# Down's seven products in another order, the residual loaded in two parts, and one row of steps through gate, up and down

## The chip, the cores and the metric

One core of one Trainium2 chip runs the whole program. The metric is the device time of one execution in microseconds (us). Before the change it is 1949.96 us, the median of three runs (1948.24 to 1951.97).

## The reference, cut to what matters

The program is one layer of a hybrid encoder trunk, with 1024 tokens, 1024 channels and a feed-forward width of 4096. Three mixers and a first layer norm make x1. All that this document is about comes behind that:

```
x  = layer_norm(ALPHA * x + mix @ w_out, ln1_g, ln1_b)          # x1
ff = square(relu(x @ w_up)) @ w_down                            # up, down
pe = sigmoid(x @ w_pe_gate) * (p @ w_pe_proj)                   # gate
x  = layer_norm(ALPHA * x + ff + pe, ln2_g, ln2_b)              # output
```

## The kernel before

**Arithmetic.** Every float32 operand of a matmul is split in two parts, hi (written by ScalarE, L1204 or L866) and lo (the rest, a subtraction in `split_lo`, L116, on VectorE or GpSimd). `three` (L983) then makes three matmuls of one product: hi with hi, hi with lo, lo with hi (L986 to L988). Gate, up and down are each cut in 2x2 blocks and computed with seven block products in place of eight, numbered 1 to 7. Their operands are sums and differences of blocks, their results accumulate in PSUM. Products 1, 6, 7, 4 add up in one set of four banks (`al_`, tag "m"), products 2 and then 5, 3 in the other (`be_`, tags "pj" and "fj"). A running sum is read after each product, before the next product may write its bank. The eight banks are these two sets.

**Gate** (`pg_prep`, `pg_mm`, L1031 to L1082): the products in the order 1, 2, 5, 6, 7, 4, 3, four steps each. Product 5 leaves its sum of weights in a tile `sc` that products 6 and 3 read again (L1037). When a block is done, `pg_fin` loads two tiles (L1001, L1003), takes the sigmoid, multiplies, adds the residual and stores to `xr_d` (L1007). The stage's working tiles lie in the pool "pg".

**Up** (`up_load`, `up_prep`, `up_mm`, L1090 to L1172): 16 column pairs j of 256 columns, seven products each, of 12 matmuls. The raw weights of an even j go into two slots of the general pool (30 slots of 4 KB), those of an odd j into the tile "wur" of a pool "ff" (L1093), which takes the memory of "pg" once the tiles there are released. Results are squared and stored to `h_d` (L1132).

**Down** (`operands`, `down_prep`, `down_mm`, L1178 to L1301): two chunks `ch` of the width, seven products each in the order of the gate, four steps u each, of 24 matmuls, so 96 matmuls a product. `operands` loads raw tiles (six buffers) or cached ones (slots), combines them on VectorE (1024 elements wide) and splits them into hi and lo tiles, of which there are three buffers each; only the last product of the last chunk (`final`) has slots of its own for them and does its matmuls token tile by token tile. After a product `acc` (L1246) adds the four banks to the residual tiles `x2`, in the second chunk with `bn_stats` (L1296) where a half row is complete, and `ln2_t` does the layer norm of a token tile: GpSimd (L190), ScalarE (L1254), four VectorE operations (L1255, L1256), two stores (L1257). All eight `x2` tiles are loaded by the first step of the first product 2 (L1265).

**What sets the order.** Each stage calls `ahead` (L1022), which issues the preparation of step i+3 (gate, up) or i+2 (down) before the matmuls of step i, and ends before the next stage begins. The framework then fixes each engine's order at compile time, by the order of the code and by a model of time, so that a later instruction can be moved ahead of an earlier one that the model sees waiting. On the chip every engine's queue runs in that fixed order. All transfers are issued by SyncE's queue (SPq).

```python
    ahead([(lambda n=n, k=k: pg_prep(n, k), lambda w, n=n, k=k: pg_mm(n, k, w)) for n in ORDER for k in range(4)], 3)
    ff = phase("ff", "tile")
...
    ahead([(lambda j=j, n=n: up_prep(j, n), lambda w, j=j, n=n: up_mm(j, n, w)) for j, n in steps2], 3)
...
    dn = phase("down", "tile")
```

Of the kernel before, what the change touches and what calls it, by code (L numbers as in the profile page):

```python
# [15 lines left out]
P = 128  # L16
# [38 lines left out]
def hybrid_block(ctx, tc, x, xT, pT, w_in, relb, conv_w, conv_b, cln_g, cln_b, dnw, a_log, dt_bias,  # L55
# [975 lines left out]
    def pg_prep(n, k):  # L1031
        if n == 1:
            w = gload(0, 0, k, n)
        elif n == 2 or n == 3:
            w = gload(1, 0, k, n)
            if n == 3:
                V.tensor_tensor(w, w, sc[k], ALU.subtract)  # L1037
        elif n == 5:
            a, b = gload(0, 1, k, n), gload(1, 1, k, n)
            w = sc[k] = pg([P, 512], F32, "sc", 4, "sc")  # L1040
            V.tensor_tensor(w, a, b, ALU.add)
        elif n == 6:
            a = gload(0, 0, k, n)
            w = sc[k]
            V.tensor_tensor(w, w, a, ALU.subtract)
        elif n == 7:
            a, w = gload(0, 0, k, n), gload(0, 1, k, n)
            V.tensor_tensor(w, a, w, ALU.subtract)
        else:
            w = gload(1, 1, k, n)  # L1050
        return hilo(w, f"wg{n}{k}", G if k % 2 else V)
# [27 lines left out]
                pg_fin(4 + t, 0, u2[t])  # L1079

    ORDER = (1, 2, 5, 6, 7, 4, 3)
    ahead([(lambda n=n, k=k: pg_prep(n, k), lambda w, n=n, k=k: pg_mm(n, k, w)) for n in ORDER for k in range(4)], 3)  # L1082


    ff = phase("ff", "tile")
    v4 = lambda a: a.rearrange("p (k c) -> p k c", c=P)
    upo, upa, upb, upc, upr = {}, {}, {}, {}, {}
    NP = DFF // 256

    def up_load(j):  # L1090
        if j >= NP:
            return
        raw = [slot([P, 4, 256], name=f"wu{j}{q}") if j % 2 == 0 else ff([P, 4, 256], F32, "wur", 2, f"wu{j}{q}")  # L1093
               for q in range(2)]
        for q in range(2):
            SY.dma_start(raw[q], wview(w_up, 4 * q, 4, 256 * j, 256))
        upo[j] = (raw[0][:, :, 0:P], raw[1][:, :, 0:P], raw[0][:, :, P:256], raw[1][:, :, P:256])

    ss_ = {}

    def up_prep(j, n):
        a11, a12, a21, a22 = upo[j]
        if n == 1:
            up_load(j + 1)
            src, eng = a11, V
        elif n == 2:
            src, eng = a12, G
        elif n == 4:
            src, eng = a22, G
        else:  # L1110
            t = lraw(f"s{n}")
            src, eng = v4(t), G if n in (6, 3) else V
            if n == 5:
                V.tensor_tensor(src, a21, a22, ALU.add)
                ss_[j] = src
            elif n == 6:
                V.tensor_tensor(src, ss_[j], a11, ALU.subtract)
                ss_[j] = src
            elif n == 7:
                V.tensor_tensor(src, a11, a21, ALU.subtract)  # L1120
            else:
                V.tensor_tensor(src, a12, ss_[j], ALU.subtract)
        hi, lo = hilo(src, f"wu{n}", eng, v4)
        return [(v4(hi)[:, k, :], v4(lo)[:, k, :]) for k in range(4)]

    def ustage(name):
        return ff([P, 512], F32, "st", 10, name)

    def hstore(j, i, hf, v):
        f = 2 * j + i  # L1130
# [34 lines left out]
            steps += [(j + 1, 1), (j + 1, 2)]  # L1165
        steps += [(j, 4), (j, 3)]

    up_load(0)
    steps2 = []
    for j, n in steps:  # L1170
        steps2.append((j, {6: 5, 5: 6}.get(n, n)))
    ahead([(lambda j=j, n=n: up_prep(j, n), lambda w, j=j, n=n: up_mm(j, n, w)) for j, n in steps2], 3)  # L1172
    scoped[0].close()
    scoped[0] = None
    late.close()


    dn = phase("down", "tile")  # L1178
    x2 = [None] * NT

    def dt4(dt, tag, bufs, name):
# [7 lines left out]
    def bload(dst, g, i, j):  # L1189
        SY.dma_start(dst, wview(w_down, 4 * g + 2 * i, 2, 512 * j, 512))  # L1190
        return dst

    def raw():
        return dt4(F32, "raw", 6, "draw")

    def cache(name):
        return slot([P, 2, 512], name=name)

    def hilo4(src, which, final):
        if final:  # L1200
            hi, lo = [slot([P, 2, 512], F32R, name=which + x) for x in "hl"]
        else:
            hi, lo = [dt4(F32R, which + x, 3, which + x) for x in "hl"]
        S.activation(hi, src, AF.Copy)  # L1204
        split_lo(V, lo, src, hi)
        return hi, lo
# [52 lines left out]

    ADDS = {1: [(0, 0)], 2: [(0, 0)], 5: [(1, 1)], 6: [(0, 1)], 7: [(1, 1)], 4: [(1, 0)], 3: [(0, 1)]}  # L1260
    def down_prep(ch, n, u):
        if (ch, n, u) == (0, 2, 0):
            for t in range(NT):
                x2[t] = slot([P, D], name=f"x2_{t}")
                SY.dma_start(x2[t], xr_d[t])  # L1265
        if (ch, n, u) == (1, 1, 0):
            rows.extend([load_rows(ln2_g), load_rows(ln2_b)])
        return operands(n, 4 * ch + u, (ch, n) == (1, 3))

    rows, held = [], []  # L1270

    def down_mm(ch, n, u, ab):
# [2 lines left out]
        if n in (2, 5) and u == 0:  # L1275
            be_[:] = [bank(ALT[t], name="pdb") for t in range(4)]
        bs = al_ if n in (1, 6, 7, 4) else be_
        final = (ch, n) == (1, 3)
        if final:
            held.append(ab)  # L1280
        else:
# [7 lines left out]
        for t in range(4):  # L1289
# [2 lines left out]
                    for k in range(2):  # L1292
                        three(bs[t], part(a, k, t), part(b, k), False, v == 3 and k == 1)
            acc(4 * i + t, c, bs[t])
            if ch == 1 and n in (2, 7, 4, 3):
                V.bn_stats(lst[4 * i + t][:, c, :], x2[4 * i + t][:, 512 * c:512 * c + 512])  # L1296
                if n in (4, 3):
                    ln2_t(4 * i + t, *rows)

    ahead([(lambda ch=ch, n=n, u=u: down_prep(ch, n, u), lambda ab, ch=ch, n=n, u=u: down_mm(ch, n, u, ab))  # L1300
           for ch in range(2) for n in ORDER for u in range(4)], 2)  # L1301
    scoped[0].close()


# [37 lines left out]
```

## Time and profile before

| | us |
|---|---|
| median of 3 runs | 1949.96 |
| the profiled execution, its own time | 1944.56 |
| its span, first to last instruction | 1942.8 |
| gate, up and down with the last layer norm, in that span | about 1169 to 1943 |
| up's first matmul | 1275.2 |
| down's first matmul | 1601.0 |

The profiled execution lies 0.28% under the median of the runs. Times in the rows are microseconds from the span's start. A matmul's own time is longer than the distance to the next, since matmuls overlap; lengths of products are therefore taken from start to start. In the names, pga and pgb are the two bank sets in gate, pua, pub and puc the banks in up, pda (`al_`) and pdb (`be_`) the sets in down.

### The profile page before, as it was taken

The page shows a single profiled execution, that of the slowest core. Times are in us where ns is not written, and L with a number is a line of the kernel's source. Part 1 is how long each engine was busy: PE and PEld are TensorE (multiplying, and loading weights), DVE is VectorE, ACT ScalarE, POOL GpSimd, SP SyncE. Part 2 cuts the span into 40 slices and gives each one's busy share as a digit, 9 for nine tenths or more (in the row PEclk, how much of TensorE's full clock was granted, in tenths as well). Part 3 has the DMA queues.
Part 4 walks back from the last instruction along what each step waited for, and adds up shares of the span by engine and source line. Part 5 has one row for each costly group of instructions (what it writes and reads, how often), then busy time and mean ns, then how long its engine had stood idle before and what let it go on. Part 6 is the DMA issues. An engine that isn't in the chain of part 4 may idle for free. (4 is left out here: it accounts for less than half of the span.)

```text
span 1942.8 us, 25812 instructions
## 1 busy us (share of the span) xinstructions
PE 1850.1 (95%) x9265; PEld 1543.4 (79%) x9265; DVE 1258.3 (65%) x2203; ACT 831.1 (43%) x1516; POOL 445.0 (23%) x373
## 2 busy tenths in 40 slices
PE   8999999989999989989999999989999989999996
PEld 7988887778777878777877997768888877878775
DVE  3248969989957857664377367763333327865978
ACT  4454544446324343442344237435555553333333
POOL 2123423334322122212121142223232310000001
PEclk9999999999999989999999999999999999999998
DMA  6212222232242332333354435763333367542442
GB/s 200 82 53 68 74 64 72 65 87 87 87 117 60 98 90 84 92 111 107 125 190 163 155 123 188 246 211 130 104 114 108 109 233 251 214 162 97 175 152 87
DMA packets 207793, 244.68 MB, mean 126 GB/s; under 512 B 23792, under 2 KB 126256, under 8 KB 207664
## 3 DMA queue, kind: packets, MB, share of 16 engines
q1 hardware_dynamic: 207664, 243.03, 38.6%
q8 instruction: 73, 1.20, 0.2%
q14 instruction: 56, 0.46, 0.1%
HBM read 183.17 MB, written 59.80 MB: 125 GB/s over the span
## 5 line engine op out<-in xcount | busy, mean ns | idle before, releaser
L676 DVE SCALAR_TENSOR_TENSOR ca<-ci,cw_s,ca 128x512 f32<-128x512 f32 x240 | 214.2, 892 | 3.8
L986 PE MATMUL pda<-bh,ah 128*128 128x512 f32 x256 | 97.6, 396 | 9.1 <-DVE x L1246 5.1
L987 PE MATMUL pda<-bl,ah 128*128 128x512 f32 x256 | 100.6, 393 | 0.0
L988 PE MATMUL pda<-bh,al 128*128 128x512 f32 x256 | 100.4, 393 | 0.0
L190 POOL TENSOR_TENSOR mv<-mv,nhalf 128x1 f32<-128x1 f32 x16 | 17.4, 1094 | 360.9 <-DVE mv L683 360.9
L307 POOL TENSOR_SCALAR st<-st,mx 128x640 f32<-128x640 f32 (+2 forms) x64 | 58.7, 919 | 179.8 <-DVE mx L306 174.2
L304 ACT ACTIVATE st<-st,mx 128x640 f32<-128x640 f32 (+2 forms) x64 | 44.5, 696 | 117.0 <-DVE mx L300 116.8
L986 PE MATMUL pdb<-bh,ah 128*128 128x512 f32 x192 | 74.6, 401 | 7.0 <-DVE x L1246 7.0
L1204 ACT ACTIVATE ah<-draw 128x1024 fp32r<-128x1024 f32 x32 | 33.9, 1061 | 102.9 <-PE pda L987 51.2
L1157 DVE TENSOR_TENSOR r<-puc,r 128x512 f32<-128x512 f32 x16 | 11.1, 692 | 103.1 <-PE puc L988 103.1
L987 PE MATMUL pdb<-bl,ah 128*128 128x512 f32 x192 | 76.4, 398 | 0.0
L988 PE MATMUL pdb<-bh,al 128*128 128x512 f32 x192 | 75.9, 398 | 0.0
L986 PEld LDWEIGHTS pda<-bh,ah 128*128 128x128 f32 x256 | 48.6, 190 | 20.9 <-ACT bh L1204 7.3
L988 PEld LDWEIGHTS pda<-bh,al 128*128 128x128 f32 x256 | 48.7, 190 | 10.4
L987 PEld LDWEIGHTS pda<-bl,ah 128*128 128x128 f32 x256 | 48.7, 190 | 10.2 <-DVE bl L116 0.2
L553 DVE TENSOR_TENSOR tm<-X 32x31 f32<-32x31 f32 (+15 forms) x124 | 53.4, 431 | 3.0
L116 DVE TENSOR_TENSOR al<-draw,ah 128x1024 fp32r<-128x1024 f32 x32 | 39.1, 1221 | 22.7 <-ACT ah L1204 22.7
L431 DVE SCALAR_TENSOR_TENSOR c<-pc,dnw_s,c 128x511 f32<-128x511 f32 (+2 forms) x72 | 52.5, 731 | 0.1
L554 DVE TENSOR_TENSOR X<-X,tm 32x31 f32<-32x31 f32 (+15 forms) x124 | 50.1, 404 | 3.0
L771 ACT ACTIVATE sgl<-sgl 128x512 f32<-128x512 f32 x48 | 30.2, 631 | 50.0 <-DMA sgl<-sg_d 41.5
L334 ACT ACTIVATE ph<-tp 128x512 fp32r<-128x512 f32 (+2 forms) x72 | 37.0, 525 | 32.0 <-PE tp L330 27.5
L116 POOL TENSOR_TENSOR wu2l<-wu,wu2h 128x512 fp32r<-128x512 f32 x16 | 20.8, 1303 | 128.1 <-ACT wu2h L866 128.1
(1605 smaller groups left out, 6199.7 us busy)
## 6 DMA issues: line engine op xcount, KB each, us to landing
draw<-h_d SPq DMA_DIRECT2D x48, 512.0 KB, 5.0
wu<-in_w_up_dram SPq DMA_DIRECT2D x32, 512.0 KB, 3.9
h_d<-r SPq DMA_DIRECT2D x64, 256.0 KB, 2.1
draw<-in_w_down_dram SPq DMA_DIRECT2D x32, 512.0 KB, 4.6
sg_d<-fs SPq DMA_DIRECT2D x48, 256.0 KB, 2.1
sgl<-sg_d SPq DMA_DIRECT2D x48, 256.0 KB, 2.8
wg<-in_w_pg_dram SPq DMA_DIRECT2D x36, 256.0 KB, 4.3
cb<-in_w_down_dram SPq DMA_DIRECT2D x16, 512.0 KB, 8.1
```

What stands on the lines that cost most here:

```text
L116: eng.tensor_tensor(lo, src, hi.bitcast(F32), ALU.subtract)
L304: S.activation(st[:, :nk], st[:, :nk], AF.Exp, scale=-1.0, bias=mx[:, nm:nm + 1], accum_out=mx[:, 2:3])
L307: G.tensor_scalar(st[:, :nk], st[:, :nk], mx[:, 3:4], 1.0, ALU.mult, ALU.mult)
L334: S.activation(ph[:, :n], tp[:, :n], AF.Copy)
L431: V.scalar_tensor_tensor(acc[:, 512 * hf + s_:512 * hf + 512], pp[:, :512 - s_], cw[:, 3 - s_:4 - s_], acc[:, 512 * hf + s_:512 * hf + 512 ...
L553: V.tensor_tensor(tv, bc_last(L, ncol), bc_mid(R, nr), ALU.mult)
L554: V.tensor_tensor(X3[:, jj + 1:32, 0:ncol], X3[:, jj + 1:32, 0:ncol], tv, ALU.subtract)
L676: V.scalar_tensor_tensor(acc, t[:, H - s_:H - s_ + 512], cw_s[:, i, H - s_:KB - s_], acc, ALU.mult, ALU.add)
L986: PE.matmul(out_, lhsT=ah, rhs=bh, start=first, stop=False, skip_group_check=True)
L987: PE.matmul(out_, lhsT=ah, rhs=bl, start=False, stop=False, skip_group_check=True)
L988: PE.matmul(out_, lhsT=al, rhs=bh, start=False, stop=last, skip_group_check=True)
L1204: S.activation(hi, src, AF.Copy)
```

## The change

- Down's products come in the order 2, 1, 5, 6, 3, 7, 4. So the last one, with slots of its own, is product 4 in place of 3; the layer norm of token tiles 0 to 3 follows product 3, that of tiles 4 to 7 follows product 4.
- Residual tiles 0 to 3 are loaded by the first step of product 1, tiles 4 to 7 by the third step of product 5.
- The three calls of `ahead` become one row of steps: preparations of up are issued during gate's last steps, those of down during up's last. Up loses its pool "ff": "wur" moves into "pg" and shares its two buffers of 4 KB with gate's `sc` (two `sc` tiles in each), its staging tiles use "st" of "pg", with 12 buffers in place of 10.
- Down's pool is opened only when it is first needed. The first two steps of product 2 in chunk 0 take raw, hi and lo tiles from the general slots.

```diff
         elif n == 5:
             a, b = gload(0, 1, k, n), gload(1, 1, k, n)
-            w = sc[k] = pg([P, 512], F32, "sc", 4, "sc")
+            if k % 2 == 0:
+                sc[k] = pg([P, 1024], F32, "wur", 2, "sc")
+                sc[k + 1] = sc[k][:, 512:]
+                sc[k] = sc[k][:, :512]
+            w = sc[k]
...
-    ff = phase("ff", "tile")
...
-        raw = [slot([P, 4, 256], name=f"wu{j}{q}") if j % 2 == 0 else ff([P, 4, 256], F32, "wur", 2, f"wu{j}{q}")
+        raw = [slot([P, 4, 256], name=f"wu{j}{q}") if j % 2 == 0 else v2(pg([P, 1024], F32, "wur", 2, f"wu{j}{q}"))
                for q in range(2)]
...
     def up_prep(j, n):
+        if n == 1:
+            if j == 0:
+                up_load(0)
+            up_load(j + 1)
...
-        return ff([P, 512], F32, "st", 10, name)
+        return pg([P, 512], F32, "st", 12, name)
...
+    dnp = []
+
+    def dn(*a):
+        if not dnp:
+            scoped[0].close()
+            scoped[0] = None
+            late.close()
+            dnp.append(phase("down", "tile"))
+        return dnp[0](*a)
...
+    first = [False]
+
     def raw():
-        return dt4(F32, "raw", 6, "draw")
+        return cache("raw") if first[0] else dt4(F32, "raw", 6, "draw")
...
-        if (ch, n, u) == (0, 2, 0):
-            for t in range(NT):
+        if ch == 0 and (n, u) in ((1, 0), (5, 2)):
+            for t in range(4 if n == 5 else 0, 8 if n == 5 else 4):
                 x2[t] = slot([P, D], name=f"x2_{t}")
                 SY.dma_start(x2[t], xr_d[t])
-        if (ch, n, u) == (1, 1, 0):
+        if (ch, n, u) == (1, 3, 0):
             rows.extend([load_rows(ln2_g), load_rows(ln2_b)])
-        return operands(n, 4 * ch + u, (ch, n) == (1, 3))
+        first[0] = (ch, n) == (0, 2) and u < 2
+        return operands(n, 4 * ch + u, (ch, n) == (1, 4) or (ch, n) == (0, 2) and u < 2)
...
-        final = (ch, n) == (1, 3)
+        final = (ch, n) == (1, 4)
...
-            if ch == 1 and n in (2, 7, 4, 3):
+            if ch == 1 and n in (1, 7, 4, 3):
...
+    flow = [([(3, lambda _, n=n, k=k: pg_prep(n, k))], lambda w, n=n, k=k: pg_mm(n, k, w))
+            for n in ORDER for k in range(4)]
+    flow += [([(3, lambda _, j=j, n=n: up_prep(j, n))], lambda w, j=j, n=n: up_mm(j, n, w)) for j, n in steps2]
+    flow += [([(2, lambda _, ch=ch, n=n, u=u: down_prep(ch, n, u))], lambda ab, ch=ch, n=n, u=u: down_mm(ch, n, u, ab))
+             for ch in range(2) for n in (2, 1, 5, 6, 3, 7, 4) for u in range(4)]
+    made = {}
+    for i in range(-4, len(flow)):
+        for lead in (4, 3, 2):
+            if 0 <= i + lead < len(flow):
+                for l, f in flow[i + lead][0]:
+                    if l == lead:
+                        made[i + lead] = f(made.get(i + lead))
+        if i >= 0:
+            flow[i][1](made.pop(i))
```

## Rows read from the trace of the kernel before

**Rows 1.** The page: an engine's busy time, share of the span, instructions.

```profile
PE 1850.1 (95%) x9265; PEld 1543.4 (79%) x9265; DVE 1258.3 (65%) x2203; ACT 831.1 (43%) x1516; POOL 445.0 (23%) x373
```

**Rows 2.** Waits of PE, 1150 to 1943: waiter, releaser, us in total, times, longest.

```profile
PE pua L986 <- ACT wu1h L866: 7.9, 1, 7.9
PE pdb L986 <- DVE x L1246: 7.0, 2, 3.8
PE pda L986 <- DVE x L1246: 5.1, 4, 2.4
PE pda L986 <- ACT bh L1204: 4.0, 1, 4.0
...
PE pub L986 <- DVE u L1078: 1.4, 1, 1.4
```

**Rows 3.** Windows: up's first five products; one later. Busy (count) by engine, PEclk, DMA.

```profile
1275.20:1300.48 25.28, 15.98 (x62) 12.31 (x60) 13.36 (x20) 6.68 (x12) 1.10 (x1) 0.86 0.66 217
1569.89:1572.64 2.75, 2.75 (x14) 2.25 (x13) 0.00 (x0) 0.60 (x1) 1.30 (x1) 1.00 0.92 240
```

**Rows 4.** Timeline of up's beginning: start, us, engine, line, tiles [idle before].

```profile
1290.69 0.68 DVE L1157 TENSOR_TENSOR r<-pub,r 128x512 f32<-128x512 f32 x1
1291.22 2.11 SPq L1096 DMA_DIRECT2D wu<-in_w_up_dram  x2
1291.41 0.63 ACT L1158 ACTIVATE r<-r 128x512 f32<-128x512 f32 x1 [7.91 <-DVE r L1157]
...
1295.24 0.63 ACT L866 ACTIVATE wu1h<-wu 128x512 fp32r<-128x512 f32 x1 [2.54 <-DMA wu<-in_w_up_dram]
...
1297.36 0.63 PE L986 MATMUL pua<-xc1h,wu1h 128*128 128x512 f32 x1
...
1297.79 0.63 PE L987 MATMUL pua<-xc1l,wu1h 128*128 128x512 f32 x1
```

**Rows 5.** Line 1037, gate's last reads of sc: ns min/median/max, first and last start.

```profile
L1037 DVE TENSOR_TENSOR wg<-wg,sc x4: 692/692/694, 1244.7 to 1249.7; 128x512 f32<-128x512 f32 x4
```

**Rows 6.** SyncE's queue, timeline of up's end: the residual's loads.

```profile
1572.60 6.51 SPq L1265 DMA_DIRECT2D x<-xr_d  x6
```

**Rows 7.** Windows of down, PE product starts (1; 2; 5+6; 7; 3; 2; 5+6; 7; 4+3).

```profile
1601.02:1625.58 24.56, 24.56 (x96) 20.02 (x97) 14.91 (x15) 9.79 (x11) 0.00 (x0) 0.88 0.54 191
1625.58:1650.67 25.09, 21.92 (x97) 17.86 (x96) 21.54 (x21) 10.02 (x10) 0.00 (x0) 1.00 0.89 307
1650.67:1696.79 46.12, 45.41 (x193) 37.10 (x193) 40.17 (x40) 14.86 (x15) 0.00 (x0) 0.96 0.59 215
1696.79:1721.27 24.48, 22.04 (x97) 17.94 (x97) 16.29 (x17) 9.15 (x10) 0.00 (x0) 1.00 0.54 182
...
1743.15:1764.91 21.76, 21.76 (x98) 18.02 (x96) 12.18 (x13) 8.05 (x9) 0.00 (x0) 1.00 0.15 50
...
1786.67:1812.41 25.74, 21.92 (x97) 17.86 (x96) 21.44 (x21) 10.02 (x10) 0.00 (x0) 0.98 0.88 310
1812.41:1859.89 47.48, 46.79 (x192) 37.93 (x193) 42.54 (x44) 14.84 (x15) 0.00 (x0) 0.94 0.28 97
1859.89:1883.15 23.26, 22.02 (x96) 17.94 (x97) 16.38 (x17) 8.58 (x10) 0.00 (x0) 1.00 0.54 184
1883.15:1926.85 43.70, 43.70 (x192) 35.93 (x192) 41.08 (x68) 17.81 (x21) 4.14 (x5) 1.00 0.21 69
```

**Rows 8.** Window from the end of the last product 7 to VectorE's last instruction.

```profile
1882.30:1939.20 56.90, 43.86 (x192) 35.96 (x192) 54.22 (x97) 23.11 (x28) 5.90 (x8) 0.93 0.26 91
```

**Rows 9.** VectorE's timeline in that window: neighbours of 1024 and of 512 elements.

```profile
1898.43 1.22 DVE L116 TENSOR_TENSOR bl<-draw,bh 128x1024 fp32r<-128x1024 f32 x1
1899.57 1.22 DVE L116 TENSOR_TENSOR bl<-cb,bh 128x1024 fp32r<-128x1024 f32 x1
...
1921.96 0.67 DVE L1255 TENSOR_TENSOR x<-x,lnp 128x512 f32<-128x512 f32 x1
1922.55 0.68 DVE L1256 TENSOR_TENSOR x<-x,lnp 128x512 f32<-128x512 f32 x1
```

More of the change, by code (lines that the diff above doesn't have):

```diff
@@ L1081, in hybrid_block @@
     ORDER = (1, 2, 5, 6, 7, 4, 3)
-    ahead([(lambda n=n, k=k: pg_prep(n, k), lambda w, n=n, k=k: pg_mm(n, k, w)) for n in ORDER for k in range(4)], 3)
-    ff = phase("ff", "tile")
     v4 = lambda a: a.rearrange("p (k c) -> p k c", c=P)
+    v2 = lambda a: a.rearrange("p (k c) -> p k c", c=256)
     upo, upa, upb, upc, upr = {}, {}, {}, {}, {}
@@ L1101, in up_prep @@
     def up_prep(j, n):
+        if n == 1:
+            if j == 0:
+                up_load(0)
+            up_load(j + 1)
         a11, a12, a21, a22 = upo[j]
         if n == 1:
-            up_load(j + 1)
             src, eng = a11, V
@@ L1166, in hybrid_block @@
         steps += [(j, 4), (j, 3)]
-    up_load(0)
     steps2 = []
@@ L1171, in hybrid_block @@
         steps2.append((j, {6: 5, 5: 6}.get(n, n)))
[L1172 to L1178, printed above, removed]
+    dnp = []
[6 more added lines that the diff above has]
+        return dnp[0](*a)
     x2 = [None] * NT
@@ L1191, in bload, with hilo4 @@
         return dst
+    first = [False]
     def raw():
-        return dt4(F32, "raw", 6, "draw")
+        return cache("raw") if first[0] else dt4(F32, "raw", 6, "draw")
     def cache(name):
         return slot([P, 2, 512], name=name)
-    def hilo4(src, which, final):
-        if final:
+    def hilo4(src, which, own):
+        if own:
             hi, lo = [slot([P, 2, 512], F32R, name=which + x) for x in "hl"]
@@ L1298, in down_mm @@
                     ln2_t(4 * i + t, *rows)
-    ahead([(lambda ch=ch, n=n, u=u: down_prep(ch, n, u), lambda ab, ch=ch, n=n, u=u: down_mm(ch, n, u, ab))
-           for ch in range(2) for n in ORDER for u in range(4)], 2)
+    flow = [([(3, lambda _, n=n, k=k: pg_prep(n, k))], lambda w, n=n, k=k: pg_mm(n, k, w))
[12 more added lines that the diff above has]
+            flow[i][1](made.pop(i))
     scoped[0].close()
```

## The prediction

> **What bounds the kernel now.** I read the page first: PE is busy 95% of the span [rows 1], so time can only come from its waits, or from matmuls that run at the lower clock. The changed stages begin at about 1169 us, so the second view is PE's waits behind that. Five of them lie in places that the change touches [rows 2]: 7.9 and 1.4 us where up begins, 4.0 where down begins, and 12.1 in down (7.0 and 5.1) in which PE waits for `acc` to read a bank that the next product writes. The third view is the windows, because a wait also costs what comes after it. One product of up takes 2.75 us when nothing disturbs it [rows 3], one of down 21.76 us [rows 7]; what a stretch takes above that is its loss, the low clock included.
>
> At up's beginning the cause is in order of time [rows 4]: SyncE issues the loads of the second column pair at 1291.2, behind all loads and stores of gate's `pg_fin`, because their memory was part of gate's pool; ScalarE can split them at 1295.2, and PE then runs at 0.43 us from matmul to matmul, the lower level of 1.2 GHz, where 0.23 is usual. At down's beginning nothing is missing but memory: the operands were loaded, their hi and lo tiles lie where up's tiles lay.
>
> **The change part by part.** The sum is made against the profiled execution, 1944.56 us, which stands 5.4 us below the median of the runs; I carry the difference over to the median.
>
> (a) Up's beginning. The first five products take 25.28 us where 5 x 2.75 = 13.75 would do [rows 3]: a loss of 11.5. The loads of pair 1 now need only the memory of `sc`, whose last reader starts at 1249.7 [rows 5]. They are issued some 40 us earlier, two of 512 KB, and nothing stands behind their wait on SyncE's queue for longer than that subtraction. What is late next: product 2 of pair 0 still waits 1.4 us for gate's banks [rows 2], and product 7 of pair 0 waits for a copy that stands on ScalarE behind L1158 and one square, so it comes at 1291.4 + 3 x 0.63 = 1293.3 [rows 4]. With the five products in a row from 1279.5 (pair 0's 2, 5, 6, pair 1's 1, 2), PE is there at 1279.5 + 13.75 = 1293.25. So 1.7 us stays and 9.8 go. Bounds: 2 gained (the splits of pair 1 queue behind L1157, at 1290.7, and little but the load's wait goes) to 11.5 (all).
>
> (b) Down's beginning. The wait of 4.0 [rows 2] and the first product's 24.56 - 21.76 = 2.8 [rows 7] are 6.8 us. The first two steps now have tiles of their own in slots that up's finished operands free, so they can be ready before up ends. They give PE 2 x 5.44 us; within them the third step's raw tiles must land and be split. Late next is one bank that up's last product leaves to a VectorE read of 0.68 [rows 4], while three others are free. I take the whole 6.8; bounds 3 to 6.8.
>
> (c) Chunk 0. The bank conflicts in the old order are 2 to 5, 6 to 7 and 7 to 4; in the new one 2, 1, 5, 6, 3, 7 each find their bank set unused for a whole product, and only 7 to 4 is left. Losses now: 25.09 - 21.76 = 3.3 (product 2, waiting for the bank at its end), 46.12 - 43.52 = 2.6 (5 and 6: low clock behind that wait, and the wait before 7), 24.48 - 21.76 = 2.7 (7, waiting before 4) [rows 7]. 2.7 stays, 5.9 go. Bounds 3 to 8.6.
>
> (d) Chunk 1, products before the last two. 25.74 - 21.76 = 4.0 and 47.48 - 43.52 = 4.0 [rows 7]: 7.9 go. Bounds 5 to 7.9. Its wait from 7 to 4 (23.26 - 21.76 = 1.5) stays and is counted in (e).
>
> (e) The end. From 1882.3, when the last product but two is done, to the span's end at 1942.8 are 60.5 us, and VectorE is busy 54.2 of the first 56.9 [rows 8]: here it is VectorE that sets the end, not PE, which has only two products (43.70 us) [rows 7] to do. The change does not take an operation from it. From the end of product 3 it has the same list: 16 operations of 1024 elements, 1.14 apart, and about 56 of 512, 0.6 apart, with small ones [rows 9], in all 54 us. What changes is the order. In the code four layer norms (each four operations of 0.6 and three small ones, some 2.7 us) now stand ahead of product 4's twelve splits and subtractions, which PE needs; the old order had half its norms behind all splits. Strictly in the code's order, product 4's last operands are ready after 15.6 (adds, statistics and norms of product 3: 4 x 3.9) + 4.5 (four splits of product 7) + 13.6 (12 x 1.14) + 4.8 (product 7's adds and statistics) + 3 of waits = 41.5 us. PE then still has up to 78 matmuls to do, 17.7 us, and the last tile's norm takes some 8 by my estimate, with 3.6 from VectorE's last instruction to the span's end [rows 8]: 71, a loss of 10. If the norms only fill gaps, PE ends after 43.5 + 1.5 and the end comes at 57: a gain of 4. The nearest row is the old end, where the planner put the splits first; I take a loss of 2.
>
> **Costed at nothing.** The number of loads does not change. Residual tiles 0 to 3 are needed at product 2's end, 21.8 us into down, tiles 4 to 7 two products later; today six issues pass SyncE's queue within 6.5 us during up [rows 6], whose stores they hardly delay. If that cover is gone, `acc` waits on VectorE with the next splits behind it, which two steps of lead (10.9 us) absorb.
>
> Sum: -9.8 - 6.8 - 5.9 - 7.9 + 2.0 = -28.4. On the profiled execution 1916.2, against the median **1921.6, say 1922 us**.
>
> **A rule weighed.** Where one product follows another on the other bank set, from 4 to 3, PE loses nothing: product 3 takes 21.76 us at a granted clock of 1.00 [rows 7]. The Trainium skill, TensorE: Matmul & The Clock Gate, "A second HAM failure mode: psum-queue depth-cycling", warns against what the new order does more often: a kernel that cycled through banks in PSUM lost throughput to brief idling between groups of matmuls and a clock that fell and rose. By that rule part of (c) and (d) would be given back; the row is against it.
>
> **The rivals.**
> - *The norms starve product 4* (the strict order of (e)): 10 lost in place of 2, 1930 us. For it: norms come first in the code. Against it: while ScalarE and GpSimd have a norm in hand, VectorE is free for splits.
> - *Up's beginning stays late*: VectorE's and ScalarE's queues are late next, not the load. (a) gives 2, so 1929 us. For it: ScalarE idles 7.9 us for VectorE [rows 4].
> - *The one row does nothing*: the planner already moves work ahead (the residual's loads run during up [rows 6]), and both seams stay. (a) and (b) are gone: 1922 + 16.6 = 1938 us.
> - *Each change of bank set costs*, as the low clock does behind a wait for a bank: (2.6 - 0.7) in chunk 0 and (4.0 - 0.7) in chunk 1 [rows 7], 2.6 in the mean. Eleven changes are 28.6: 1950 us, no change. For and against it is what the paragraph above says.
> - *Slower*: VectorE starves PE in chunk 1's products 7 and 4 at every step, and PE stays at 1.2 GHz for both. Deficit: 38.5 us of VectorE work (15.6 + 4.5 + 13.6 + 4.8) against some 26 of PE (product 7 and the first tile of 4), 13; and 192 matmuls at 0.43 in place of 0.23, 38.4. In place of the 2 that makes 51: 1971 us. It decides once stalls and low clock pass 30 us, with 13 of stalls from some 85 of the 192 matmuls. For it: behind today's waits the clock is down (0.88 over a product) [rows 7]. Against it: it rose again within that product each time, since operands were there.
>
> **How the numbers follow.** Forecast 60%, norms first 18%, late up 8%, seams stay 5%, bank sets 2%, slower 6%, and 1% for what I have not thought of, put with no change. Only the forecast's own bounds reach far down: all gains at their best are 42, which together is unlikely, so the range begins at 1912. It ends at 1938, with the seams that stay. A measurement of this kernel can tell about 0.2%, 3.9 us. Faster by more: 60 + 18 + 8 + 5 = 91%; within it 3%; slower 6%.
>
> **What would show it.** (a) right: no wait of PE for wu1h, first five products of up in about 15.5 us. (b): no 4 us gap, first product of down near 21.8. (c), (d): `acc` named as PE's releaser only before product 4; 2 to 5 gone. (e): VectorE busy nearly all of the last 60 us, PE with a wait for product 4's splits. A wait of PE of over 5 us in products 7 or 4, or a granted clock under 0.9 there, would make the forecast wrong; so would a PE gap over 4 us at either seam.

## The result and the profile after

The changed kernel takes **1930.41 us** (median of four runs, 1929.69 to 1931.43) beside 1949.85 us before (median of four runs, one more than above; 1948.24 to 1951.97): a ratio of 0.99, 95% interval 0.9883 to 0.9917, so 16 to 23 us less. It lies inside the range of the prediction, 8.4 us above its 1922: 28 us were forecast, 19.4 came.

| us | before | after |
|---|---|---|
| median of the runs | 1949.85 | 1930.41 |
| profiled execution, its own time | 1944.56 | 1930.17 |
| span | 1942.8 | 1928.2 |
| gate's last matmul ends | 1275.4 | 1277.2 |
| up's last matmul ends | 1597.0 | 1597.1 |
| last matmul of the kernel ends | 1927.0 | 1916.8 |

The profiled execution of before stood 5.4 us under its median, that of after stands on its own. So the two traces differ by 14.4 us only. Of these, gate gives back 1.8, and it is not shown to be the change's doing: in the profiles of the experiments below, gate's last matmul ends anywhere from 1274.3 to 1286.1 us in kernels that have the same gate as after or, in e11_x1_bufs, nearly so. So I compare behind gate's last matmul: 667.4 us before, 651.0 after, **16.5 us less**. Against these the steps are counted.

PE's waits from 1150 us on, in the columns of [rows 2]:

```profile
PE pda L986 <- DVE x L1258: 8.3, 2, 4.4
PE pdb L986 <- ACT bh L1216: 5.5, 1, 5.5
PE pub L986 <- DVE u L1082: 2.2, 1, 2.2
...
PE pda L987 <- DVE bl L116: 1.2, 1, 1.2
```

The wait of 7.9 us for wu1h is gone, and of the six waits for `acc` (L1246 before, L1258 now) two are left, both between products 7 and 4. But down's beginning has a longer wait than before (5.5 for 4.0), in its third step in place of its first. The wait of 1.2 us for bl is in product 7 of chunk 1.

Windows of after, in the columns of [rows 3, 7]: up's first five products; down's first 60 matmuls behind up (and two of the next product); chunk 0's products 7 and 4; chunk 1's product 1; its 5 and 6; and from product 7 to the span's end:

```profile
1277.08:1294.82 17.74, 15.58 (x61) 12.33 (x60) 14.33 (x19) 7.36 (x14) 5.10 (x3) 0.90 0.88 302
1597.84:1619.89 22.05, 16.52 (x62) 13.13 (x63) 14.26 (x13) 9.40 (x11) 0.00 (x0) 0.85 0.91 322
1706.48:1755.76 49.28, 45.39 (x194) 37.12 (x192) 34.10 (x35) 16.07 (x17) 0.00 (x0) 0.97 0.56 184
1777.52:1799.28 21.76, 21.76 (x98) 18.02 (x96) 19.50 (x20) 8.05 (x9) 0.00 (x0) 1.00 0.69 250
1799.28:1842.80 43.52, 43.52 (x194) 36.05 (x192) 38.66 (x42) 16.09 (x17) 0.00 (x0) 1.00 0.07 20
1864.56:1928.20 63.64, 46.62 (x193) 37.42 (x191) 58.36 (x100) 23.55 (x28) 8.21 (x8) 0.89 0.38 133
```

A product of up takes 2.75 us undisturbed and one of down 21.76 (0.227 us a matmul). The first row loses 17.74 - 13.75 = 4.0 (11.5 before), the second 22.05 - 62 x 0.227 = 8.0, the third 49.28 - 43.52 = 5.8. The fourth and fifth lose nothing, where before 4.0 and 4.0 were lost [rows 7].

Down's beginning in the trace, SyncE's queue (SPq), ScalarE and PE:

```profile
1592.46 7.00 SPq L1138 DMA_DIRECT2D h_d<-r  x3
1599.55 0.39 SPq L1196 DMA_DIRECT2D draw<-h_d  x1
1600.04 0.45 SPq L1200 DMA_DIRECT2D draw<-in_w_down_dram  x1
...
1603.99 1.06 ACT L1216 ACTIVATE ah<-draw 128x1024 fp32r<-128x1024 f32 x1 [4.87 <-DMA draw<-h_d]
1605.32 1.06 ACT L1216 ACTIVATE bh<-draw 128x1024 fp32r<-128x1024 f32 x1 [0.27 <-DMA draw<-in_w_down_dram]
...
1606.43 2.07 PE L986 MATMUL pdb<-bh,ah 128*128 128x512 f32 x4 [5.53 <-ACT bh L1216]
```

The third step's loads stand on the queue behind up's last three stores of h, which wait there until 1599.46 for the tiles that they store. ScalarE idles 4.87 us for them, PE 5.53. And of the 48 matmuls of the first two steps, meant as cover, 36 had run already between up's last products, from 1572.2 to 1591.4, in place of up's small waits for `r`.

VectorE between products 7 and 4 of chunk 0: the split for product 4's second step, product 4's last subtraction, the four accumulations.

```profile
1727.76 1.22 DVE L116 TENSOR_TENSOR bl<-draw,bh 128x1024 fp32r<-128x1024 f32 x1
1730.32 1.23 DVE L1247 TENSOR_TENSOR draw<-draw,ct 128x1024 f32<-128x1024 f32 x1 [1.34 <-DMA draw<-in_w_down_dram]
1731.46 2.47 DVE L1258 TENSOR_TENSOR x<-pda,x 128x512 f32<-128x512 f32 x4
```

The accumulations, for which PE stands 3.89 us, queue behind the subtraction for product 4's fourth step, which PE comes to 3 x 5.44 us after the first, and which itself waits 1.34 us for its load. (PE began product 7's last step at 1722.80 without a wait, so all splits behind that are product 4's.)

Before the last product 4, in chunk 1, the accumulations stand behind product 4's subtractions and splits and among the norms' scalings (L1267):

```profile
1888.08 1.22 DVE L1247 TENSOR_TENSOR draw<-draw,ct 128x1024 f32<-128x1024 f32 x1
...
1889.81 1.22 DVE L116 TENSOR_TENSOR bl<-draw,bh 128x1024 fp32r<-128x1024 f32 x1
1890.95 0.68 DVE L1267 TENSOR_TENSOR x<-x,lnp 128x512 f32<-128x512 f32 x1
1891.55 0.68 DVE L1258 TENSOR_TENSOR x<-pda,x 128x512 f32<-128x512 f32 x1
```

### The profile page after: what moved, and what is told of

Same layout as the page of the kernel before. It is cut to its first block, busy times and chain, and to the rows that moved or that the text cites. A ratio compares the mean times of both kernels' runs of the same rounds, so it can differ in the third digit from the quotient of the medians.

```text
span 1928.2 us, 25795 instructions
## 1 busy us (share of the span) xinstructions
PE 1848.2 (96%) x9265; PEld 1545.3 (80%) x9265; DVE 1254.8 (65%) x2203; ACT 831.8 (43%) x1516; POOL 449.9 (23%) x373
## 5 line engine op out<-in xcount | busy, mean ns | idle before, releaser
L986 PEld LDWEIGHTS pda<-bh,ah 128*128 128x128 f32 x256 | 49.1, 192 | 19.2 <-ACT x L1266 4.8
L987 PEld LDWEIGHTS pda<-bl,ah 128*128 128x128 f32 x256 | 49.1, 192 | 11.9 <-DVE bl L116 1.7
L431 DVE SCALAR_TENSOR_TENSOR c<-pc,dnw_s,c 128x511 f32<-128x511 f32 (+2 forms) x72 | 52.5, 731 | 0.1
L986 PEld LDWEIGHTS pdb<-bh,ah 128*128 128x128 f32 x192 | 36.4, 190 | 14.6 <-ACT bh L1216 6.0
```

The costliest lines, as they stand in the source:

```text
L431: V.scalar_tensor_tensor(acc[:, 512 * hf + s_:512 * hf + 512], pp[:, :512 - s_], cw[:, 3 - s_:4 - s_], acc[:, 512 * hf + s_:512 * hf + 512 ...
L986: PE.matmul(out_, lhsT=ah, rhs=bh, start=first, stop=False, skip_group_check=True)
L987: PE.matmul(out_, lhsT=ah, rhs=bl, start=False, stop=False, skip_group_check=True)
```

## The experiments

Theory after the result: the change's parts work, but (1) down's beginning depends on where the third step's loads stand on SyncE's queue, (2) the two waits left in down come from the order on VectorE, not from the amount of its work, and (3) order and row of steps need each other. (The planner is the framework's scheduler, which fixes each engine's order.) In the table the "stretch" runs, in the profile, from up's last matmul to the span's end (before 345.8, after 331.1; kernels with the one row, so all but before and e1_order, have 8.2 us of down's matmuls ahead of it).

| kernel | median | before, same chip | ratio, 95% interval | stretch |
|---|---|---|---|---|
| e1_order | 1945.75 | 1947.73 | 0.9985, 0.9974 to 0.9996 | 343.3 |
| e2_row | 1937.70 | 1947.73 | 0.9941, 0.9923 to 0.9960 | 336.4 |
| e3_raw_slots | 1925.20 | 1947.73 | 0.9888, 0.9866 to 0.9909 | 329.8 |
| e6_norm_after | 1932.61 | 1947.73 | 0.9908, 0.9889 to 0.9927 | 334.9 |
| e5_raw7 | 1933.96 | 1947.65 | 0.9921, 0.9899 to 0.9944 | 335.1 |
| e7_no_norm | 1925.26 | 1947.65 | 0.9878, 0.9854 to 0.9901 | 327.7 |
| e8_acc_first | 1927.51 | 1947.65 | 0.9894, 0.9870 to 0.9918 | 327.2 |
| e9_one_part | 1929.47 | 1947.65 | 0.9909, 0.9885 to 0.9932 | 333.6 |
| e10_all | 1924.52 | 1951.68 | 0.9862, 0.9845 to 0.9878 | 322.3 |
| e11_x1_bufs | 1930.06 | 1951.68 | 0.9888, 0.9873 to 0.9902 | 332.3 |
| e12_pool_norm | 1928.39 | 1951.68 | 0.9871, 0.9849 to 0.9893 | 324.7 |
| e13_end_order | 1918.14 | 1946.53 | 0.9850, 0.9830 to 0.9870 | 321.9 |

The ratio is an estimate from all runs and not the quotient of the two medians. The executions of one kernel spread by some 10 us here, so what separates kernels by few us is read from the stretch and its waits.

The stretch has a part that moves without an edit. From the last product 7 to the span's end it takes 63.6 us in after and 63.3 in e11_x1_bufs, but 65.0 to 65.7 in e3_raw_slots, e5_raw7, e8_acc_first, e9_one_part and e10_all, whose end has the same code. In these five VectorE's order is another: in e8_acc_first four and in e10_all three of the norms' multiplications and additions (0.6 us each) stand between the last accumulation and its statistics, in after none. So some 2 us of a stretch can be this order, and each edit is judged by the window that it aims at.

**The order alone.**

```diff
...
-           for ch in range(2) for n in ORDER for u in range(4)], 2)
+           for ch in range(2) for n in (2, 1, 5, 6, 3, 7, 4) for u in range(4)], 2)
```

> The kernel before with the new order of down's products alone (2, 1, 5, 6, 3, 7, 4, with the last product, the norms' rows and the moments moved to fit); gate, up and down keep their three separate rows of steps, and all eight parts of the residual are loaded at down's first step. Theory (the parts lean on each other): the bank waits of down's second half go (7.9 us) and 2.9 us of the first half's, the end costs 2.7 us more, but down now begins with product 2, whose four raw tiles of each step come late behind eight residual loads: down's beginning stays at 24.5 us or gets up to 5 us worse. Sum -3 to -8 us, so 1942 to 1947 against 1950. Rival (the parts are independent, down's beginning doesn't mind which product is first): -8 us. Rival (the single row of steps brings nearly all of the gain): within 2 us of the kernel before, with bank waits as before.

Its gain is 1 to 5 us, at the edge of what was expected. The time alone would also fit the last rival, but the bank waits went as in after (chunk 1 loses nothing, chunk 0 5.7), but down's beginning got 4.3 us worse: 11.2 us are lost in it, 6.9 before.

```profile
1590.21 12.39 SPq L1132 DMA_DIRECT2D h_d<-r  x4
1602.70 0.37 SPq L1186 DMA_DIRECT2D draw<-h_d  x1
...
1609.29 1.22 PE L986 MATMUL pdb<-bh,ah 128*128 128x512 f32 x2 [9.09 <-ACT bh L1204]
```

Product 2's raw tiles lie in down's pool, so their loads go out behind four stores of up and PE waits 9.09 us. Product 1, first in the old order, loads into slots.

**The row alone.**

```diff
...
-             for ch in range(2) for n in (2, 1, 5, 6, 3, 7, 4) for u in range(4)]
+             for ch in range(2) for n in ORDER for u in range(4)]
```

(The cut lines load the residual in one part at product 2 and give the slots for hi and lo tiles to the first two steps of product 1.)

> The changed kernel with down's old order of products (1, 2, 5, 6, 7, 4, 3) and the residual in one part at the first step of product 2; the one row of steps stays. Theory: the gain in up stays (7.5 us at its first five products, 2.7 in its last ones), down's beginning is judged by what its third step waits for: its tiles for product 1 are slots of the cache, free from the start, so their loads can go out ahead of up's last stores of h, the wait of 5.5 us at down's third step goes and 5 to 7 us are gained there; the bank waits are as in the kernel before. Sum -14 to -18 us: 1932 to 1936. Rival (the third step waits for something else than loads queued behind up's stores, such as the splits on ScalarE and VectorE): the 5.5 us wait stays, -9 to -11 us: 1939 to 1941.

Measured 8 to 15 us less than before, in the median (1937.7) between the theory and the rival. The mechanism held: with product 1 first all loads of its four steps are out by 1586.6, the third step's split follows up's last square on ScalarE at once, at 1603.44, and the 5.5 us wait fell to 1.3 and 1.4.

```profile
1586.16 0.42 SPq L1200 DMA_DIRECT2D cb<-in_w_down_dram  x1
...
1602.90 0.63 ACT L1137 ACTIVATE r<-r 128x512 f32<-128x512 f32 x1
1603.44 1.04 ACT L1216 ACTIVATE ah<-ca 128x1024 fp32r<-128x1024 f32 x1
```

```profile
PE pda L987 <- DVE bl L116: 1.4, 1, 1.4
PE pda L986 <- ACT bh L1216: 1.3, 1, 1.3
```

```profile
1601.31:1620.92 19.61, 16.97 (x62) 13.11 (x60) 12.07 (x12) 9.21 (x11) 0.00 (x0) 0.83 0.88 314
```

The size did not: 60 matmuls still take 19.61 us for 13.6, at a granted clock of 0.83, so PE ran at 1.2 GHz for part of them behind two short waits. Order alone and row alone gave 2.9 and 11.5 us (ratios times 1949.85), both together 19.4; behind gate's last matmul the traces show 1.2, 10.6 and 16.5. By the intervals (1 to 5, 8 to 15, 16 to 23) the surplus over the sum is not clear of noise. That the order needs the row, which gives product 2 slots and lead, is read from the traces: down's beginning, where e1_order waits 9.09 us.

**All raw tiles of the first product in slots.**

```diff
-        first[0] = (ch, n) == (0, 2) and u < 2
+        first[0] = (ch, n) == (0, 2)
```

> The changed kernel, with the raw tiles of all four steps of down's first product (not of two) in slots that are free before up ends, so that SyncE issues the third and fourth step's loads ahead of up's last stores of h. Theory (down's third step waits for loads that stand on SyncE behind those stores): the wait of PE for bh of 5.53 us at down's third step falls under 1 us, the low clock behind it goes, 5 to 7 us less than the changed kernel: 1923 to 1926. Rival (the split tiles' buffers or ScalarE's work set it): the loads land earlier, the wait stays at 3 us or more, under 2 us less. Rival (the loads now collide with up's stores or delay them): up's last products wait, no gain.

The loads of down's first product in the trace (count, ns, first and last start), and PE's window over its last 60 matmuls:

```profile
L1200 SPq DMA_DIRECT2D raw<-in_w_down_dram x4: 386/420/422, 1562.3 to 1576.2; - x4
L1196 SPq DMA_DIRECT2D raw<-h_d x3: 360/371/408, 1569.2 to 1575.7; - x3
```

```profile
1601.71:1619.16 17.45, 15.96 (x61) 12.36 (x61) 11.21 (x10) 8.97 (x11) 0.00 (x0) 0.90 0.83 307
```

```profile
PE pdb L987 <- DVE bl L116: 1.3, 1, 1.3
```

They are out before 1577 where the third step's went out at 1599.6. The wait for bh is gone (0.2 us; 1.3 us for bl is left), the loss is 17.45 - 13.6 = 3.8 for after's 8.0. That is the theory, a little short of 5 us (the median, 1925.2, lies in its band), and it repeats: the four kernels with this edit lose 2.4 to 4.7 us in these 60 matmuls, the seven with the one row, the new order and without it 7.5 to 8.5. The stretch is only 1.3 us shorter than after's, since products 7 and 4 of chunk 0 lose 7.0 us here for 5.8 and the end 1.6 more.

The edit gives the loads other memory as well as another place on the queue. That the place counts can be read in after's trace: what the first of the third step's loads waits for had been set by 1588 (for its memory, GpSimd's last instruction, at 1575.3), and it went out at 1599.55. The load for bh, at 1600.04, waits also for PE, at the latest for up's last matmul at 1597.1. So at least 2.9 us of its delay are the queue's; how much of the rest is the memory's is not shown.

**The accumulations of chunk 0 first.**

```diff
-            V.tensor_tensor(b, b, ct[g], ALU.subtract)
+            with tc.issue_after(done7[0]) if g in (2, 3) else ExitStack():
+                V.tensor_tensor(b, b, ct[g], ALU.subtract)
...
```

(`done7` is product 7's last accumulation in chunk 0; what the block issues queues behind it on its engine.)

> The changed kernel with VectorE's subtractions for product 4's third and fourth steps, in down's first half, queued behind product 7's four accumulations instead of ahead of them. Theory B (the wait of 3.9 us between products 7 and 4 there is the order on VectorE): the wait falls to 1.5 us or less, the low clock behind it goes too, 2.5 to 5 us less: 1925.5 to 1928. Theory A (buffers and loads set it; the splits of product 7 stand ahead as well): the wait stays over 2.5 us. Rival (the put-off subtractions starve product 4's later steps): a new wait of 1 to 3 us for bl at its third or fourth step, and no gain.

```profile
1723.61 2.73 DVE L1259 TENSOR_TENSOR x<-pda,x 128x512 f32<-128x512 f32 x4
1726.26 2.35 DVE L1248 TENSOR_TENSOR draw<-draw,ct 128x1024 f32<-128x1024 f32 x2
```

```profile
1703.69:1747.21 43.52, 43.52 (x194) 36.04 (x192) 33.67 (x35) 16.20 (x17) 0.00 (x0) 1.00 0.64 205
```

Products 7 and 4 on the same banks now take 43.52 us: nothing is lost at all, 5.8 gained, and no wait came in its place; the median, 1927.5, lies in theory B's band. This too repeats: in the four kernels with this edit nothing is lost there, in the seven with the new order, the one row and without it 5.8 to 8.9 us. (The stretch is 3.9 us shorter than after's, since the end takes 65.2 us for 63.6.) The rival that one more buffer would do it was tried beside it:

```diff
-        return cache("raw") if first[0] else dt4(F32, "raw", 6, "draw")
+        return cache("raw") if first[0] else dt4(F32, "raw", 7, "draw")
```

> The changed kernel with seven raw buffers for down's loads instead of six. In the changed kernel VectorE's subtraction for product 4's fourth step waits 1.34 us for its load, with product 7's four accumulations queued behind it, and PE stands 3.89 us between products 7 and 4 of down's first half. Theory A (that load was late because a raw buffer came free late): with a seventh buffer the load is early, the accumulations come 1 to 3 us sooner, the wait falls to 1 to 2.5 us: 1927.5 to 1929.5. Theory B (the planner's order on VectorE is what counts, it puts the subtractions ahead of the accumulations whatever the loads do): the wait stays within 1 us of 3.9, time within 1.5 us of the changed kernel's 1930.4.

```profile
1727.77 1.22 DVE L1247 TENSOR_TENSOR draw<-draw,ct 128x1024 f32<-128x1024 f32 x1 [2.56 <-DMA draw<-in_w_down_dram]
...
1731.18 2.47 DVE L1258 TENSOR_TENSOR x<-pda,x 128x512 f32<-128x512 f32 x4
```

```profile
PE pda L986 <- DVE x L1258: 9.5, 2, 5.8
```

Both expectations missed: the wait grew from 3.9 to 5.8 us. All four subtractions stood ahead of the accumulations, three of them after 2.5 us of waiting for their loads. The order decides, and one more buffer doesn't mend it; why the loads came later with it stays open.

**The residual in one part.**

```diff
-        if ch == 0 and (n, u) in ((1, 0), (5, 2)):
-            for t in range(4 if n == 5 else 0, 8 if n == 5 else 4):
+        if (ch, n, u) == (0, 1, 0):
+            for t in range(NT):
```

> The changed kernel with all eight parts of the residual loaded at one place (the first step of product 1) instead of four there and four at product 5. Theory (the four loads fit beside up's last products, where the queue has room, but they stand ahead of the loads for down's third step): the wait of 5.5 us at down's third step grows by 0 to 3 us: 1930 to 1934. Rival (the split is what holds down's beginning together): the wait grows by 5 us or more, 1936 to 1940. Rival (the second part's place costs the third step nothing and hinders product 5): 1 to 2 us faster, 1928.5 to 1929.5.

```profile
PE pdb L986 <- ACT bh L1216: 5.6, 1, 5.6
```

The wait at the third step is 5.6 us for 5.5. The median, 1929.47, falls in the last case's band, but the runs spread by 9.6 us. The split of the residual's loads does nothing that these runs can show.

**Up's beginning.**

```diff
-        xr = pg([P, 512], F32, "x1", 2, "x1")
+        xr = pg([P, 512], F32, "x1", 4, "x1")
```

> The changed kernel with four buffers instead of two for the input x that the gate's finish reads. In the changed kernel VectorE stands 1.85 us and 0.69 us for a load of x just before gate's last accumulations, which stand behind it, and PE waits 2.16 us for their bank in up's first products. Theory (the two buffers of x make those loads late): the wait of PE for u of gate falls under 1 us, the low clock after it goes, 2 to 4 us less: 1926.5 to 1928.5. Rival (VectorE's own work ahead of the accumulations is enough to make them late): the wait stays at 1.5 us or more, time within 1.5 us of 1930.4. Rival (the loads of x, issued sooner, delay the loads of up's weights): a wait for wu of 1 us or more in up's first products, no gain.

The first rival's numbers came: the wait for gate's bank was 1.55 us, the time 1930.06. With two buffers the wait was none in e12_pool_norm, 1.47 in e10_all, 1.8 in e13_end_order and 3.2 in e3_raw_slots. So the buffers are not shown to matter. Nor are late loads ruled out: VectorE no longer waits for x there, but for pp, which still has two buffers, just before the first of gate's last accumulations:

```profile
1281.57 0.69 DVE L1005 TENSOR_TENSOR u<-pp,u 128x512 f32<-128x512 f32 x1 [1.46 <-DMA pp<-pp_d]
1282.18 0.68 DVE L1082 TENSOR_TENSOR u<-pgb,u 128x512 f32<-128x512 f32 x1
```

What makes this wait vary stays open.

**The end.** Edits of VectorE's work behind product 3, first with the norms of tiles 0 to 3 behind the last split:

```diff
+        if final:
+            with tc.issue_after(last[0].ins):
+                for t in range(4):
+                    ln2_t(t, *rows)
...
-                if n in (4, 3):
+                if n == 4:
```

> The changed kernel with the norms of tiles 0 to 3 (VectorE's aggregates, scales and shifts) queued behind the last split of down's last product, instead of between its splits. Theory (in the changed kernel the accumulation that product 4 waits for stands behind the norms and the splits): PE's wait of 4.4 us between products 7 and 4 falls to 1 to 2 us, product 4 ends 3 to 5 us sooner; but VectorE has the same 54 us of work in the last 60 us, so the end itself gains 0 to 3 us: 1927.5 to 1930.5. Rival (the wait is a bank conflict that any order has): wait and time as in the changed kernel, within 1 us. Rival (norms put off pile up behind product 4, VectorE then ends later): 1 to 4 us slower, 1931.5 to 1934.5.

```profile
PE pda L986 <- DVE x L1259: 5.9, 2, 4.0
```

The third case came: PE's wait fell from 4.4 to 1.9 us (5.9 less chunk 0's 4.0), but the stretch grew by 3.8, and the time stands at 1932.6. Here the norms' aggregates were put off too, and what was put off came at the end.

```diff
-            V.tensor_tensor(x2[t][:, sl], x2[t][:, sl], lg[:, sl], ALU.mult)
+            if rest:
+                V.tensor_tensor(x2[t][:, sl], x2[t][:, sl], lg[:, sl], ALU.mult)
```

(the addition of `lb` likewise; `rest` is t > 3.)

> The changed kernel without the scale and shift that VectorE does for tiles 0 to 3 in the last norm (sixteen instructions of 0.6 us, 9.6 us of VectorE's work in its last 60 us); it leaves that part of the output out. Theory (the end is bound by VectorE's work): PE's waits between products 7 and 4 fall from 4.4 us to 1 to 2 us, and the end comes 4 to 8 us sooner: 1922.5 to 1926.5. Rival (the end is the chain product 4's last bank, its norm, its store, and the norms of tiles 0 to 3 only fill idle time of VectorE): only the PE wait goes, 2 to 3 us: 1927.5 to 1928.5. Rival (neither): within 1 us of 1930.4.

The median falls in the theory's band, the trace between the two: from product 7 to the span's end it takes 60.5 us for 63.6, so 9.6 us less of VectorE's work bring 3.1. PE still waits 3.0 before product 4; the profile names a ScalarE instruction for it, but PE starts 0.8 us behind VectorE's first accumulation, at 1886.3.

**Two edits together, and two more at the end.** e10_all joins e3_raw_slots and e8_acc_first; e12_pool_norm adds this, e13_end_order another order instead:

```diff
-            V.tensor_tensor(x2[t][:, sl], x2[t][:, sl], lb[:, sl], ALU.add)
+            (G if t < 4 else V).tensor_tensor(x2[t][:, sl], x2[t][:, sl], lb[:, sl], ALU.add)
```

```diff
-            with tc.issue_after(done7[0]) if g in (2, 3) else ExitStack():
+            with tc.issue_after(done7[0]) if g in (2, 3, 7) else ExitStack():
...
+        if final:
+            with tc.issue_after(last4[0]):
+                for t in range(4):
+                    ln2_end(t, *rows)
```

(In e13_end_order `last4` is the last split, `ln2_end` the scale and shift of a tile, and `done7` is set in both chunks.)

> The changed kernel with two of the edits tried singly: all raw tiles of down's first product in slots, and in down's first half the subtractions for product 4's third and fourth steps behind product 7's accumulations. Theory (the two waits are independent, each with its own cause): PE's wait at down's third step under 1.5 us and no wait between products 7 and 4 of the first half; 4 us and 5.7 us of PE's time saved, so 8 to 10 us less than the changed kernel: 1920.5 to 1922.5. Rival (what is gained at down's beginning is waited for at the next products, since the loads of the first half are the bound): one of the two waits comes back by 2 us or more, or another of over 2 us stands in the first half, 1923 to 1927.

> The two edits of e10_all, and the last addition of the norm (the shift) of tiles 0 to 3 on GpSimd instead of VectorE, eight instructions, some 0.6 us each on VectorE (4.8 us) and, by GpSimd's splits of the same size, some 1.3 to 1.7 us there. Theory (the end is bound by VectorE's work): against e10_all, the wait between the last products 7 and 4 falls from 4.4 us to 3 us and the end comes 2 to 4 us sooner: 1917.5 to 1920. Rival (the end is the chain of product 4's last banks, norm and store): within 1 us of e10_all. Rival (GpSimd's work slows VectorE's beside it, or tiles 0 to 3 end late): 1 to 4 us slower than e10_all.

> The two edits of e10_all, and VectorE's order at the end set by hand: the split for product 4's last step behind product 7's accumulations, and the scale and shift of tiles 0 to 3 behind that split (their aggregates stay early). No work is added or taken away. In e10_all PE waits 4.51 us between the last products 7 and 4, and the stretch from product 7's first matmul to the end of the span takes 65.7 us. Theory (there it is the order on VectorE, not the amount of its work, that costs): the wait falls to 2 us or less and the stretch to 61.5 to 63.5 us, so 2 to 4 us less than e10_all: 1920.5 to 1922.5. Rival (VectorE's amount of work is the bound: what is put off comes at the end, as in e6_norm_after): the wait falls, the stretch stays at 65 us or more, 1923.5 to 1927.

```profile
PE pda L986 <- DVE x L1259: 4.5, 1, 4.5
PE pdb L987 <- DVE bl L116: 1.5, 1, 1.5
```

In e10_all both waits are gone (1.5 us for bl is left at down's beginning), and the stretch is 8.8 us shorter than after's (4.2 and 5.8 were to be had): the causes are independent. At the end 2.1 us more are lost than in after, as in the other kernels with the other order there. The median is 2 us above the theory's band and inside the rival's, though no wait came back; its before is 1.8 to 5.2 us slower than the others.

e12_pool_norm is not faster: the third case came by the medians (3.9 us slower than e10_all, the intervals overlap) and by the trace, in which PE's wait before the last product 4 grew from 4.5 to 6.9 us. VectorE's groups around that wait (count | busy us, mean ns | idle before), of e10_all and then of e12_pool_norm:

```profile
L1270 DVE TENSOR_TENSOR x<-x,lnp 128x512 f32<-128x512 f32 x8 | 5.4, 680 | 0.0
```

```profile
L1270 DVE TENSOR_TENSOR x<-x,lnp 128x512 f32<-128x512 f32 x8 | 9.6, 1215 | 0.0
...
L1259 DVE TENSOR_TENSOR x<-pda,x 128x512 f32<-128x512 f32 x4 | 2.7, 678 | 0.0
```

Beside GpSimd's additions the multiplications took 1215 ns in the mean for 680; the accumulations, which read a PSUM bank and one tile, stayed at 678. So 4.2 us of the 4.8 that were to be saved went there, and two splits beside the additions took 1.9 and 1.7 us for 1.2.

In e13_end_order PE waits 1.86 us before product 4, and VectorE keeps the order that was set:

```profile
1876.49 1.88 DVE L1260 TENSOR_TENSOR x<-pda,x 128x512 f32<-128x512 f32 x3
...
1883.54 1.20 DVE L116 TENSOR_TENSOR bl<-draw,bh 128x1024 fp32r<-128x1024 f32 x1
1884.66 4.90 DVE L1277 TENSOR_TENSOR x<-x,lnp 128x512 f32<-128x512 f32 x8
1889.48 4.89 DVE L1278 TENSOR_TENSOR x<-x,lnp 128x512 f32<-128x512 f32 x8
...
1901.00 0.69 DVE L1260 TENSOR_TENSOR x<-pda,x 128x512 f32<-128x512 f32 x1 [2.66 <-PE pda L988]
```

```profile
1851.88:1901.00 49.12, 45.86 (x193) 36.84 (x191) 46.08 (x74) 17.66 (x20) 6.47 (x5) 0.97 0.38 129
1851.88:1912.74 60.86, 45.86 (x193) 36.84 (x191) 57.76 (x100) 23.41 (x28) 8.37 (x8) 0.92 0.37 128
```

From product 7 on, PE ends after 49.1 us, for 52.5 in e10_all; the span's end comes after 64.5 for 65.7. So 3.4 us of PE bring 1.2: most of it is the rival, VectorE busy 57.8 of 60.9 us. Its one long idle time is before the last row, at 1901.00, an accumulation that waits for PE with the norms of tiles 4 to 6 queued behind it. The stretch of 64.5 falls between the two cases, and it is longer than after's 63.6, so against the planner's better order nothing is won at the end. The median lies below both bands, beside a before that is 5 us faster than e10_all's. At 0.985 (0.983 to 0.987) this is the fastest kernel tried, faster than the change (0.99, 0.9883 to 0.9917); against e10_all the intervals overlap.

## Why the prediction was right and wrong

Its sum was -28.4; behind gate's last matmul the traces show -16.5. The measured 1930.41 is also what its rival "The norms starve product 4" gives (1930), and next to "Up's beginning stays late" (1929), but neither came: (e) lost 3.1 us and not 10, (a) gained 7.5 and not 2. The agreement is chance; the shortfall is in (a), (b) and (c).

- **(a) Up's beginning: -9.8 forecast, -7.5 measured.** The mechanism was right, wu1h's wait is gone. The term left, 1.7, was mis-sized for this trace: 4.0 are left. "Product 2 of pair 0 still waits 1.4 us" became 2.16, and product 2's twelve matmuls behind it took 4.4 us for 2.75, a low clock that was not in the sum. In the other kernels with the one row 0 to 5.0 are left (none in e12_pool_norm, 1.7 in e10_all, 5.0 in e3_raw_slots), so the size is one draw.
- **(b) Down's beginning: -6.8 forecast, about -0.4 measured.** The step that failed: "They give PE 2 x 5.44 us; within them the third step's raw tiles must land and be split." The planner spent 36 of those 48 matmuls inside up, where they brought some 2.5 us by filling waits (up takes 319.9 us with 8.2 of them in it, 321.6 before, and 7.5 went by (a)); and the third step's loads went out behind up's stores of h. Instead of 6.9 lost at this seam, 9.0 are (8.0 and 1.0 at up's last product). I had named the condition and not asked where on SyncE's queue the loads would stand. e3_raw_slots shows that earlier loads mend half of it (3.8 lost for 8.0).
- **(c) Chunk 0: -5.9 forecast, -2.9 measured.** All conflicts but 7 to 4 went, as forecast. "2.7 stays" failed: it took the old row for that pair, and 5.8 stayed, since in the new order the planner put all of product 4's subtractions and the splits of two of its steps ahead of the accumulations. e8_acc_first shows that this was neither 5.8 nor 2.7 by need, but nothing.
- **(d) Chunk 1: -7.9 forecast and measured.** Five products in a row without a loss at a granted clock of 1.00.
- **(e) The end: +2 forecast, +3.1 measured** (63.6 for the 60.5 that the prediction read). Near in size, though the planner's order alone moves it from 63.3 to 65.7, so +2.8 to +5.2. Right in cause: VectorE is busy 58.4 of 63.6 us. But the wait named for PE, "for product 4's splits", was one for the bank, with the accumulations behind splits and norms. e7_no_norm and e13_end_order are in line with the bound: neither 9.6 us less of its work nor 3.4 us less of PE's comes through in full.

These make -15.6; the 0.9 to 16.5 I don't place. The 3 us between 16.5 and the measured 19.4: the two profiled executions lie 5.3 and 0.2 us under their medians, which adds 5, and gate's 1.8 come off.

One sum of the prediction is wrong: "all gains at their best are 42" comes to 38.8 from its own bounds (11.5, 6.8, 8.6, 7.9 and 4). The range's lower end, 1912, is nearer to that.

Of its signs, the PE gap of over 4 us at a seam, said to make the forecast wrong, did come; a wait over 5 us in products 7 or 4 (3.9 and 4.4) or a clock under 0.9 there (0.97 and 0.93 until PE's end) did not. "The one row does nothing" fell: e2_row alone brings 11.5 us. "Each change of bank set costs" fell too: chunk 1's first five products change banks at each step of the order and take 21.76 us each. The Trainium skill (TensorE: Matmul & The Clock Gate, "A second HAM failure mode: psum-queue depth-cycling") tells of a kernel that cycles through PSUM banks and whose clock oscillates, by brief idling between groups of matmuls. These products show neither idling nor a low clock, so the measurement is against it here.

## What to carry to other kernels

When preparations are moved ahead across a seam, look up where each of their loads will stand on its queue: a load behind a store that waits for the stage before is as late as that stage, even where its memory is free. Matmuls that are ready early are no cover if the scheduler may spend them earlier. A wait for a bank is a matter of what stands ahead of the accumulation on its engine, so price the pair from the new order's queue, not from the old row; here one ordering edge gained 5.8 us where one more buffer gained nothing. And look whether a part that no edit touched has changed its order too, before the whole time is put down to the edit.

## What was not expected of the hardware

- GpSimd's additions of two SBUF tiles slowed VectorE's multiplications of two SBUF tiles from 680 to 1215 ns and left those that read one SBUF tile and PSUM at 678. The Trainium skill (SBUF — State Buffer, "SBUF: two separate sides") says that the two engines share a port pair as an exclusive lock, which VectorE's operations with two SBUF inputs take against GpSimd operations that read SBUF. The trace agrees: in e12_pool_norm a multiplication that starts at 1885.44, within a GpSimd addition that ends at 1886.65, ends at 1887.19.
- Waits at up's first products cost beside themselves in some traces only: behind 2.16 us (after) and 3.2 us (e3_raw_slots) product 2 took 4.4 and 4.3 us for 2.75, at the 1.2 GHz level for part of it; behind 1.5 us (e10_all) and 1.9 us (e8_acc_first) it took 2.84 and 2.83, and no more behind 2.6 us (e5_raw7, e7_no_norm). So the length of the wait alone does not decide it; what does stays open.
